# One run of value products per head pair, full-width sample products, and constant products ahead of the first slice, in a streaming encoder step

## The chip, the core and the metric

The kernel runs on one core of a Trainium2 chip. A core has a matrix engine (TensorE, shown as PE for its matmuls and PEld for its weight loads), three engines for elementwise work (VectorE or DVE, ScalarE or ACT, GpSimd or POOL) and an engine that issues transfers (SyncE or SP). TensorE reads on-chip memory and writes into PSUM, an accumulator memory of eight banks. The metric is the device time of one execution in microseconds.

## The reference

One inference step of one encoder layer, for 512 prompt frames and 64 new sample frames behind a cache of 128 frames. Width 1024, eight heads of 64 with a forget gate ("fox") and eight heads with an indexed sparse attention ("dsa"), a feed-forward width of 4096. Cut to what matters:

```python
h   = x @ w_in                       # q, k, v of both head groups, gates, index projections
# fox: s = q k^T / 8 + decay, causal, softmax, @ v
# dsa: the index heads score every key, the top 128 (sample: 48) keys are kept, softmax over them, @ v
x   = LN1(alpha * x + mix @ w_o)
x   = LN2(alpha * x + relu(x @ w_up)**2 @ w_down)
x   = x + sigmoid(x @ w_ple_gate + b) * (p @ w_ple)
```

The outputs are the new x of all frames and the new rows of the caches (k, v, log gates, index keys). The 64 sample frames attend to their 128 cached rows and to themselves: 192 keys. All of it is fp32.

## The kernel before

All activations lie transposed, features on the 128 partitions and the 576 frames (512 prompt, 64 sample) along a row. The large products are split: each fp32 operand is cast to a reduced format (fp32r, the high part), the rest is kept as a low part, and three fp32r products (high x high, low x high, high x low) take the place of one fp32 product. The function `gemm` emits these, in two halves of 288 frames; its matmuls stand at L278 for the whole kernel. The weights come by DMA in units of 512 KB, and ACT (L182) and DVE or POOL (L186) split them ahead of their use. Small products, such as transposes (L64) and the value products, are plain fp32, which the trace shows as two passes each, except for transposes, which are one.

**First stage** (`idx_main`). The inputs come in eight slices of 128 features: x (`xraw`), the index weights (`iraw`) and the first key weights (`WT.raw[0][0]`). `split_slice` casts and splits each slice on ACT, DVE and POOL (L394 to L403); then TensorE makes 6 matmuls for the first keys (L416) and 15 for the index projections (L423) per slice, 168 in all. The transfers are issued on SP in the order of the loop at L361 to L366; slice 0 comes in two halves of x.

**Attention.** The sixteen heads are worked as eight pairs: pairs 0 to 3 are fox, 4 to 7 dsa. While the projections of pair p + 1 run (`proj`, 3 units of 16 steps), the attention of pair p is woven in (`ticks`). A pair has nine jobs: for each block i of 128 queries and each of the two heads one prompt job (i + 1 key blocks), and one sample job for both heads. A job goes through the stages scores (`qk`), bias and maximum (`addmax`), exponential (`exp`), normalization, transposes of the weights (`ptrans`), their copy out of PSUM (`pevac`), value products (`pv`) and the output (`oevac`). The list `PLAN` gives each stage its lag in ticks behind the scores: `ptrans` 3, `pevac` 3, `pv` 4, `oevac` 5; within a tick the three lines of `PLAN` are separated by projection matmuls. `pv` runs only at a job that closes a group: at block 1 (queries 0 to 255: 4 products) and at block 3 (queries 256 to 511: 8 products), each into its half of the pair's PSUM bank `O` (tag "V", one buffer), and at the sample job. The transposed weights of blocks 0 and 1 lie in the tile `PT0`, those of blocks 2 and 3 in `PT1`, one buffer each.

The sample job has 64 queries of two heads, one head on each half of the partitions. Its scores are four fp32 products of 64 x 64 (L812, L813: cached and new keys, two heads), its values four products with 64 output rows (L898, L901).

Beside this, from the end of the first stage on, `choose` feeds DVE with the top-k choice of the sparse heads (logits L605 to L615, then maxima and replacements L635 and L637), until `chosen` covers pairs 4 to 7.

**Order.** The program order is that of the code; a planner in the compiler puts the instructions of each engine in order by the code's order and by when its own costs say that they are ready, and it sets the semaphores. Each engine, and each DMA queue, then runs strictly in that order.

The rest (output projection, LayerNorm, feed-forward, gate) follows from about 310 us on and is not edited.

Of the kernel before, what the change touches and what calls it, by code (L numbers as in the profile page):

```python
# [31 lines left out]
HW = NT // 2  # L32


@with_exitstack
def tile_hybrid_step(ctx: ExitStack, tc: tile.TileContext, I, O):
# [259 lines left out]

    cosT = sb.tile([128, NT], F32, name="cosT")
# [4 lines left out]
    def load_caches(g):  # L302
        KcT[g] = sb.tile([128, 4, 128], F32, name="KcT")
        Vc[g] = sb.tile([128, 512], F32, name="Vc")
        SP.dma_start(KcT[g], I["kcT"][g].rearrange("p (a t) -> p a t", a=4))
        SP.dma_start(Vc[g], I[("cache_fox_v", "cache_dsa_v")[g]][0, 0].rearrange("t h d -> t (h d)"))
# [54 lines left out]
    for a, b in ((0, 1), (1, 2), (2, 4), (4, 6), (6, 8)):  # L361
        SP.dma_start(xraw[:, a:b, :HW if a == 0 else NT], xT[:, a:b, :HW if a == 0 else NT])
        SP.dma_start(iraw[:, a:b], wix[:, a:b])
        if a == 0:
            SP.dma_start(xraw[:, 0, HW:], xT[:, 0, HW:])
        SP.dma_start(WT.raw[0][0][:, a:b], qkv[0][:, a:b])  # L366
# [284 lines left out]
    POOL.memset(zero, 0.0)  # L651
    for t in KLP:
        POOL.tensor_copy(t[64:128, 0], zero[64:128].to_broadcast([64, NP]))
        POOL.tensor_copy(t[0:64, 1], zero[0:64].to_broadcast([64, NP]))
    pair = {0: {}}

    def proj_evac(p, kind, m):
# [23 lines left out]
        if g == 0:  # L681
            if kind == "q":
                P["q32s"] = sb.tile([128, NS], F32, name="q32s", bufs=2)
# [15 lines left out]
                q(lambda: ACT.mul(P["q32s"], m[:, 1, HW - NS:HW], sc))  # L699
# [5 lines left out]
        else:  # L705
# [8 lines left out]
            if kind == "q":  # L714
                P["q32s"] = sb.tile([128, NS], F32, name="q32s", bufs=2)
                q(lambda: ACT.copy(QE[lo], x32[lo]), 5)
                q(lambda: ACT.copy(QO[hi], x32[hi]))
                q(lambda: DVE.tensor_tensor(QE[hi], x32[lo], f(QE[lo]), OP.subtract), 5)
                q(lambda: DVE.tensor_tensor(QO[lo], x32[hi], f(QO[hi]), OP.subtract))
                q(lambda: ACT.copy(P["q32s"], x32[:, NP:]))  # L720
                return
# [3 lines left out]
        P["k32s"] = sb.tile([128, NS], F32, name="k32s", bufs=2)  # L725
# [7 lines left out]
        q(lambda: ACT.copy(P["k32s"], k32[:, NP:]))  # L733
# [12 lines left out]
    def tok_out_s(src):  # L746
        m = psum_1("X", 1)
        transpose(m[:NS, 0:128], src[:, NP:], 128)
        return m
# [6 lines left out]
    def v_out(p):  # L756
        P, g = pair[p], p // 4
        m = tok_out(P["v32"])
        P["vt"] = sb.tile([128, 4, 128], F32, name="vtok", bufs=2)
        SP.dma_start(O["vT"][p // 4, p % 4], P["v32"])  # L760
        P["vs"] = sb.tile([NS, 128], F32, name="vs", bufs=2)
        ACT.copy(P["vt"], m.rearrange("p (b c) -> p b c", c=128))
        yield 1
        yield 1
        yield 1
        m = tok_out_s(P["v32"])
        ACT.copy(P["vs"], m[:NS, 0:128])

    def proj(p):
# [3 lines left out]
        for kind in "kqv" if p else "qv":  # L773
# [5 lines left out]
            if kind == "v" and p == 5:  # L779
                load_caches(1)  # L780
# [24 lines left out]
    def qk(j):  # L805
        P = pair[j["p"]]
        ps = psum_1("S", 1)
        if j["s"]:
            g, pp = divmod(j["p"], 4)
            for hh in range(2):  # L810
                r = slice(hh * 64, hh * 64 + 64)
                PE.matmul(ps[r, 0:PAST], P["q32s"][r], KcT[g][r, pp], start=True, stop=True)  # L812
                PE.matmul(ps[r, PAST:PAST + NS], P["q32s"][r], P["k32s"][r], start=True, stop=True)  # L813
# [45 lines left out]
    def ptrans(j):  # L859
        ps = psum_1("T", 1)  # L860
        j["T"] = ps
        if j["s"]:
            transpose(ps[:, 0:128], j["P"][:, 0:PAST], 128)
            transpose(ps[:NS, 128:256], j["P"][:, PAST:], 128)
        else:
            for b in range(j["i"] + 1):
                transpose(ps[:, b * 128:b * 128 + 128], j["P"][:, b * 128:b * 128 + 128], 128)
# [3 lines left out]
    def pevac(j):  # L871
        ps = j["T"]
        if j["s"]:
            t = sb.tile([128, 2, 128], F32, name="PTs")
            ACT.copy(t[:, 0], ps[:, 0:128])
            ACT.copy(t[:NS, 1], ps[:NS, 128:256])
# [3 lines left out]
        if i % 2 == 0 and hh == 0:  # L880
            pt_now["t"] = sb.tile([128, 2, 2 + 2 * (i // 2), 256], F32, name="PT", tag=f"PT{i // 2}")
        t = j["PT"] = pt_now["t"]
# [7 lines left out]
    def pv(j):  # L890
# [3 lines left out]
        if j["s"]:  # L894
            ps = j["O"] = psum_1("X", 1)
            g, pp = divmod(j["p"], 4)
            for hh, r in heads:
                PE.matmul(ps[r, :NS], Vc[g][:, (2 * pp + hh) * 64:(2 * pp + hh + 1) * 64], j["PT"][:, 0, r],  # L898
                          start=True, stop=False)
            for hh, r in heads:  # L900
                PE.matmul(ps[r, :NS], P["vs"][:, r], j["PT"][:NS, 1, r], start=False, stop=True)  # L901
            return
        i = j["i"]
        if i == 1:
            P["O"] = psum_1("V", 1)
        for kb in range(i + 1):
            c = slice(0 if kb < i else 128, 256)
            for hh, r in heads:
                PE.matmul(P["O"][r, (i - 1) * 128 + c.start:(i + 1) * 128], P["vt"][:, kb, r], j["PT"][:, hh, kb, c],  # L909
                          start=(kb == 0), stop=(kb == i))  # L910

    def oevac(j):
# [4 lines left out]
        ACT.copy(mx[:, NP:], j["O"][:, :NS])  # L917
# [167 lines left out]
    class LayerNorm:  # L1085
# [10 lines left out]
        def add(self, j):  # L1096
# [7 lines left out]
            else:  # L1104
                (DVE if j == 6 or self.sl is A else POOL).tensor_tensor(self.s, self.s, y[:, j:j + 2], OP.add)
            if j == 6:
                DVE.tensor_tensor(self.s[:, 0], self.s[:, 0], self.s[:, 1], OP.add)

# [449 lines left out]
```

## Time and profile before

| | |
|---|---|
| median of 3 runs | 798.68 us (798.48 to 799.44) |
| profiled execution | 798.88 us, span 797.2 us |
| TensorE matmuls, busy | 783.8 us (98%) |
| VectorE, busy | 539.4 us (68%) |
| ScalarE, busy | 430.3 us (54%) |
| GpSimd, busy | 119.0 us (15%) |
| DMA | 81.44 MB, mean 102 GB/s |

The span runs from the first to the last instruction that the profile shows; the execution's own time is 1.7 us longer. A TensorE share near 100% means that its instructions follow each other; how long a matmul takes from start to end is not what it costs, since matmuls overlap in the array. What one costs is read from the distance between starts.

### The profile page before, as it was taken

To read this page: it belongs to the slowest core of one execution; us is meant where nothing else is said; L and a number is where in the kernel's file an instruction comes from. 1 tells how busy PE (TensorE), PEld (TensorE's weight loads), DVE (VectorE), ACT (ScalarE), POOL (GpSimd) and SP (SyncE) were. 2 spreads that over 40 slices of the span, in tenths; PEclk is the share of its full clock that TensorE was granted. 3 is DMA by queue.
4 is the path that set the end of the run, shared out by engine and by line. 5 is a ranking of instruction groups with operands and counts; after the bars stand their busy time and mean duration, and the time that the engine had idled before them with its cause. 6 is when DMAs were issued, how large, how long until landed. Compare 5 with 4: busy or idle time off the path is not lost.

```text
span 797.2 us, 14908 instructions
## 1 busy us (share of the span) xinstructions
PE 783.8 (98%) x5886; PEld 755.7 (95%) x5886; DVE 539.4 (68%) x1100; ACT 430.3 (54%) x904; POOL 119.0 (15%) x117
## 2 busy tenths in 40 slices
PE   7999999999999999999999999999999999999997
PEld 7988898999999999999999999999999999999997
DVE  6679999644455654989856758577594765747643
ACT  5468656787677544588425427154271534616451
POOL 7202344354242000110000000000000000012200
PEclk9999999999999999999999999999999999999999
DMA  8537143354232223451313313142230513621001
GB/s 278 188 43 165 58 113 93 88 178 148 74 100 85 70 73 111 141 186 53 106 53 109 105 53 109 50 133 81 80 106 27 159 54 106 239 99 47 27 27 67
DMA packets 30358, 81.44 MB, mean 102 GB/s; under 512 B 5072, under 2 KB 9168, under 8 KB 30160
## 3 DMA queue, kind: packets, MB, share of 16 engines
q1 hardware_dynamic: 30288, 80.49, 32.9%
q8 instruction: 46, 0.75, 0.4%
q14 instruction: 24, 0.20, 0.1%
HBM read 66.38 MB, written 9.54 MB: 95 GB/s over the span
## 4 chain that ended last, share of the span: by engine, by line
PE 87%; DVE 8%; ACT 2%; DMA 1%; issue 1%; POOL 0%; SPq 0%; DVEq 0%; ACTq 0%
PE g L278 55%; PE m L278 18%; PE n L278 2%; DVE dbias L637 2%; PE V L909 2%; PE T L64 2%; DVE m L635 2%; PE S L822 1%; PE S L820 1%; PE m L416 1%; PE S L423 1%; PE X L64 1%; PE m L423 1%; DVE whl L186 1%; DVE dbias L615 1%
## 5 line engine op out<-in xcount | busy, mean ns | idle before, releaser
L182 ACT CAST whl<-wraw 128x512 fp32r<-128x512 f32 (+1 forms) x226 | 134.9, 611 | 170.7 <-PE g L278 145.6
L278 PE MATMUL g<-BH,whl 128*128 128x288 f32 (+2 forms) x864 | 181.5, 297 | 0.1
L278 PE MATMUL m<-AH,whl 128*128 128x288 f32 x736 | 178.3, 309 | 0.0
L186 DVE TENSOR_TENSOR whl<-wraw,whl 128x512 fp32r<-128x512 f32 (+1 forms) x192 | 130.0, 696 | 66.1 <-ACT whl L182 65.2
L278 PEld LDWEIGHTS g<-BH,whl 128*128 128x128 f32 x864 | 141.0, 188 | 2.3 <-ACT u L1322 1.2
L278 PEld LDWEIGHTS m<-AH,whl 128*128 128x128 f32 x736 | 126.2, 188 | 3.7 <-issue 2.2
L278 PE MATMUL g<-BL,whl 128*128 128x288 f32 (+2 forms) x432 | 127.4, 295 | 0.0
L278 PE MATMUL m<-AL,whl 128*128 128x288 f32 x368 | 109.0, 296 | 0.0
L278 PE MATMUL g<-hidE,whl 128*128 128x288 f32 (+2 forms) x768 | 103.4, 295 | 0.0
L278 PE MATMUL g<-hidO,whl 128*128 128x288 f32 (+2 forms) x768 | 103.3, 295 | 0.0
L278 PEld LDWEIGHTS g<-hidO,whl 128*128 128x128 f32 x768 | 102.3, 188 | 0.0
L278 PEld LDWEIGHTS g<-hidE,whl 128*128 128x128 f32 x768 | 102.2, 188 | 0.1
L278 PEld LDWEIGHTS g<-BL,whl 128*128 128x128 f32 x432 | 81.3, 188 | 0.1
L278 PEld LDWEIGHTS m<-AL,whl 128*128 128x128 f32 x368 | 69.5, 189 | 0.4
L278 PE MATMUL g<-s,whl 128*128 128x288 f32 x432 | 68.5, 298 | 0.0
L278 PEld LDWEIGHTS g<-s,whl 128*128 128x128 f32 x432 | 60.1, 188 | 2.2 <-DVE u L1324 1.1
L1103 POOL TENSOR_TENSOR ln_s<-Y 128x576 f32<-128x576 f32 (+2 forms) x3 | 5.0, 1665 | 381.7 <-DVE Y L1388 369.3
L838 ACT ACTIVATE sP<-sP,st 128x128 f32<-128x128 f32 (+4 forms) x72 | 39.6, 551 | 40.6 <-DVE st L830 40.2
L186 POOL TENSOR_TENSOR whl<-wraw,whl 128x512 fp32r<-128x512 f32 x34 | 44.1, 1297 | 86.8 <-ACT whl L182 68.9
L1363 DVE SCALAR_TENSOR_TENSOR Y<-Y,g 128x576 f32<-128x576 f32 x48 | 36.0, 750 | 21.7 <-PE g L278 21.2
L278 PE MATMUL m<-BH,whl 128*128 128x288 f32 x192 | 43.5, 304 | 0.0
L278 PEld LDWEIGHTS m<-BH,whl 128*128 128x128 f32 x192 | 32.1, 188 | 0.8 <-issue 0.5
(280 smaller groups left out, 1235.0 us busy)
## 6 DMA issues: line engine op xcount, KB each, us to landing
wraw<-in_w_up_dram SPq DMA_DIRECT2D x32, 512.0 KB, 3.5
wraw<-in_w_down_dram SPq DMA_DIRECT2D x32, 512.0 KB, 3.5
wraw<-in_w_qkv_dram SPq DMA_DIRECT2D x23, 512.0 KB, 3.8
wraw<-in_w_gate_dram SPq DMA_DIRECT2D x8, 512.0 KB, 4.1
wraw<-in_w_o_dram SPq DMA_DIRECT2D x8, 384.0 KB, 3.1
out_vT_dram<-v SPq DMA_DIRECT2D x8, 288.0 KB, 2.1
Y<-in_xT_dram SPq DMA_DIRECT2D x8, 288.0 KB, 5.1
PLD<-PL SPq DMA_DIRECT2D x4, 576.0 KB, 2.8
```

The source lines that it names most:

```text
L64: PE.transpose(out, in_, ident[:n, :n])
L182: ACT.copy(self.hv[h][0], src)
L186: eng.tensor_tensor(lv, src, f(hv), OP.subtract)
L278: PE.matmul(ps, W(w, kw, wc), a[:, ka, cols], start=(first and i == 0), stop=(last and i == n - 1))
L416: PE.matmul(mk[:, h, :HW], w0(part, k), a[:, k, h * HW:(h + 1) * HW], start=(k == 0 and i == 0), stop=(k == 7 and i == 2))
L423: PE.matmul(acc[b][:n[b], :304], a[:, k, b * 128:b * 128 + n[b]], ixw(part, k), start=(k == 0 and i == 0), stop=(k == 7 and i == 2))
L615: DVE.scalar_tensor_tensor(dst[:n, :nk], r[:n, :nk], w, dst[:n, :nk], op0=OP.mult, op1=OP.add)
L635: DVE.max(m, s)
L637: DVE.match_replace(out=s, in_to_replace=m, in_values=s, imm_value=GONE)
L838: ACT.activation(j["P"], j["P"], AF.Exp, bias=j["st"][:, 0:1], scale=-1.0, accum_out=s)
L909: PE.matmul(P["O"][r, (i - 1) * 128 + c.start:(i + 1) * 128], P["vt"][:, kb, r], j["PT"][:, hh, kb, c], start=(kb == 0), stop=(kb == i))
L1363: later(0, lambda y=y, m=m, s=s: DVE.scalar_tensor_tensor(y, y, s, m[:, :, :HW], op0=OP.mult, op1=OP.add))
```

## The change

Seven edits, in two groups.

*At the start:* eight fp32 products of the ones with themselves are emitted ahead of all else on TensorE, into the PSUM bank "V"; their result is not used. The transfers of slice 0's index weights and key weights are issued on ACT in place of SP.

*In the attention:*
- The prompt value products of both groups are made at block 3, as one run of 12, in place of 4 at block 1 and 8 at block 3.
- The sample scores are one product per pair: the queries of both heads stand in a 128 x 128 tile `QB` with zeros outside the two diagonal blocks, and the new keys are copied behind the cached ones in `KcT`, so that 192 keys are one operand.
- The sample values are two products of full width: the whole pair's columns of `Vc` and a 128-row tile `VS`, whose upper half is zero, against weights that are transposed 128 columns at a time. The second transpose covers keys 64 to 191; the rows of keys 64 to 127 meet the zeros of `VS`. Of the 128 x 128 result the two diagonal blocks are copied out, with one copy each.
- One copy takes both transposed blocks out of PSUM where there were two. The transpose of the sample's new values is 128 columns wide.
- `QB` and `VS` (two buffers each) are cleared once on POOL.
- `KcT` and `Vc` have two buffers, and the second cache load stands at the key unit of pair 4 in place of the value unit of pair 5.

```diff
+WARM = 8
...
+    warm = psum_1("V", 1)
+    for _ in range(WARM):
+        PE.matmul(warm[:, :128], ones, ones, start=True, stop=True)
...
     def load_caches(g):
-        KcT[g] = sb.tile([128, 4, 128], F32, name="KcT")
-        Vc[g] = sb.tile([128, 512], F32, name="Vc")
-        SP.dma_start(KcT[g], I["kcT"][g].rearrange("p (a t) -> p a t", a=4))
+        KcT[g] = sb.tile([128, 4, PAST + NS], F32, name="KcT", bufs=2)
+        Vc[g] = sb.tile([128, 512], F32, name="Vc", bufs=2)
+        SP.dma_start(KcT[g][:, :, :PAST], I["kcT"][g].rearrange("p (a t) -> p a t", a=4))
...
     for a, b in ((0, 1), (1, 2), (2, 4), (4, 6), (6, 8)):
+        other = ACT if a == 0 else SP
         SP.dma_start(xraw[:, a:b, :HW if a == 0 else NT], xT[:, a:b, :HW if a == 0 else NT])
-        SP.dma_start(iraw[:, a:b], wix[:, a:b])
+        other.dma_start(iraw[:, a:b], wix[:, a:b])
         if a == 0:
             SP.dma_start(xraw[:, 0, HW:], xT[:, 0, HW:])
-        SP.dma_start(WT.raw[0][0][:, a:b], qkv[0][:, a:b])
+        other.dma_start(WT.raw[0][0][:, a:b], qkv[0][:, a:b])
...
+    QB = [sb.tile([128, 128], F32, name=f"QB{x}") for x in range(2)]
+    VS = [sb.tile([128, 128], F32, name=f"VS{x}") for x in range(2)]
+    for t in QB + VS:
+        POOL.memset(t, 0.0)
...
-                q(lambda: ACT.mul(P["q32s"], m[:, 1, HW - NS:HW], sc))
+                q(lambda: (ACT.mul(QB[p % 2][lo, :NS], m[lo, 1, HW - NS:HW], sc),
+                           ACT.mul(QB[p % 2][hi, NS:], m[hi, 1, HW - NS:HW], sc)))
...
-                q(lambda: ACT.copy(P["q32s"], x32[:, NP:]))
+                q(lambda: (ACT.copy(QB[p % 2][lo, :NS], x32[lo, NP:]), ACT.copy(QB[p % 2][hi, NS:], x32[hi, NP:])))
...
-        q(lambda: ACT.copy(P["k32s"], k32[:, NP:]))
+        q(lambda: ACT.copy(KcT[g][:, pp, PAST:], k32[:, NP:]))
...
-        transpose(m[:NS, 0:128], src[:, NP:], 128)
+        transpose(m[:, 0:128], src[:, NT - 128:], 128)
...
-        ACT.copy(P["vs"], m[:NS, 0:128])
+        ACT.copy(VS[p % 2][NS:128], m[NS:128, 0:128])
...
-            if kind == "v" and p == 5:
+            if kind == "k" and p == 4:
                 load_caches(1)
...
-            for hh in range(2):
-                r = slice(hh * 64, hh * 64 + 64)
-                PE.matmul(ps[r, 0:PAST], P["q32s"][r], KcT[g][r, pp], start=True, stop=True)
-                PE.matmul(ps[r, PAST:PAST + NS], P["q32s"][r], P["k32s"][r], start=True, stop=True)
+            PE.matmul(ps[:, :PAST + NS], QB[j["p"] % 2], KcT[g][:, pp], start=True, stop=True)
...
-            transpose(ps[:NS, 128:256], j["P"][:, PAST:], 128)
+            transpose(ps[:, 128:256], j["P"][:, NS:PAST + NS], 128)
...
-            ACT.copy(t[:, 0], ps[:, 0:128])
-            ACT.copy(t[:NS, 1], ps[:NS, 128:256])
+            ACT.copy(t, ps[:, 0:256].rearrange("p (a c) -> p a c", a=2))
...
+            pair[j["p"]]["PT", i // 2] = pt_now["t"]
...
-            for hh, r in heads:
-                PE.matmul(ps[r, :NS], Vc[g][:, (2 * pp + hh) * 64:(2 * pp + hh + 1) * 64], j["PT"][:, 0, r],
-                          start=True, stop=False)
-            for hh, r in heads:
-                PE.matmul(ps[r, :NS], P["vs"][:, r], j["PT"][:NS, 1, r], start=False, stop=True)
+            PE.matmul(ps[:, :128], Vc[g][:, pp * 128:pp * 128 + 128], j["PT"][:, 0], start=True, stop=False)
+            PE.matmul(ps[:, :128], VS[j["p"] % 2], j["PT"][:, 1], start=False, stop=True)
             return
-        i = j["i"]
-        if i == 1:
-            P["O"] = psum_1("V", 1)
-        for kb in range(i + 1):
-            c = slice(0 if kb < i else 128, 256)
-            for hh, r in heads:
-                PE.matmul(P["O"][r, (i - 1) * 128 + c.start:(i + 1) * 128], P["vt"][:, kb, r], j["PT"][:, hh, kb, c],
-                          start=(kb == 0), stop=(kb == i))
+        if j["i"] < 3:
+            return
+        P["O"] = psum_1("V", 1)
+        for i in (1, 3):
+            t = P["PT", i // 2]
+            for kb in range(i + 1):
+                c = slice(0 if kb < i else 128, 256)
+                for hh, r in heads:
+                    PE.matmul(P["O"][r, (i - 1) * 128 + c.start:(i + 1) * 128], P["vt"][:, kb, r], t[:, hh, kb, c],
+                              start=(kb == 0), stop=(kb == i))
...
-        ACT.copy(mx[:, NP:], j["O"][:, :NS])
+        for hh in range(2):
+            r = slice(hh * 64, hh * 64 + 64)
+            ACT.copy(mx[r, NP:], j["O"][r, r])
```

More of the change, by code (lines that the diff above doesn't have):

```diff
@@ L682, in proj_evac @@
             if kind == "q":
-                P["q32s"] = sb.tile([128, NS], F32, name="q32s", bufs=2)
                 P["Q2"] = Q2[p % 2]
@@ L714, in proj_evac @@
             if kind == "q":
-                P["q32s"] = sb.tile([128, NS], F32, name="q32s", bufs=2)
                 q(lambda: ACT.copy(QE[lo], x32[lo]), 5)
@@ L724, in proj_evac @@
         P["KL"] = KL = KLP[p % 2]
-        P["k32s"] = sb.tile([128, NS], F32, name="k32s", bufs=2)
         q(lambda: ACT.copy(QE[lo], k32[lo]), 6 if g else 3)
@@ L760, in v_out @@
         SP.dma_start(O["vT"][p // 4, p % 4], P["v32"])
-        P["vs"] = sb.tile([NS, 128], F32, name="vs", bufs=2)
         ACT.copy(P["vt"], m.rearrange("p (b c) -> p b c", c=128))
```

## The prediction

> **What bounds the kernel now.** I read the page first, then the windows, then the timeline of the stretches that the change touches. The first two lines are the page's span and busy times; the other four are rows of the windows, whose columns are stretch, length, busy time and instructions of TensorE's matmuls (PE), its weight loads (PEld), VectorE (DVE), ScalarE (ACT), GpSimd (POOL), then clock, DMA share and GB/s.
>
> ```profile
> span 797.2 us, 14908 instructions
> PE 783.8 (98%) x5886; PEld 755.7 (95%) x5886; DVE 539.4 (68%) x1100; ACT 430.3 (54%) x904; POOL 119.0 (15%) x117
> 5.20:10.00 4.80, 4.71 (x17) 4.35 (x18) 3.76 (x4) 1.31 (x3) 4.35 (x6) 1.00 0.93 268
> 10.00:30.60 20.60, 20.60 (x151) 20.52 (x151) 12.93 (x16) 11.88 (x29) 12.84 (x17) 1.00 0.86 299
> 62.00:126.00 64.00, 61.19 (x454) 55.21 (x452) 62.53 (x181) 42.04 (x114) 21.27 (x19) 1.00 0.41 112
> 126.00:310.00 184.00, 184.00 (x1451) 170.92 (x1450) 102.97 (x266) 121.77 (x289) 56.54 (x46) 1.00 0.33 102
> ```
>
> TensorE is the bound, with two exceptions. From 62 to 126 us VectorE is busy for 62.5 of 64 us (the top-k choice): there TensorE waits for it now and then, and what TensorE saves is mostly lost. From 126 to 310 us TensorE is busy for all 184 us while ACT has 62 us and DVE 81 us free: there a microsecond less of TensorE is a microsecond less of the kernel. Behind 310 us nothing is edited, so that part only moves. The second exception is the clock at the start: 17 matmuls in 4.80 us (0.282 each) before 10.0 us, 151 in 20.60 (0.136 each) behind it, for the same shapes. The clock column says 1.00 in both rows; the matmul rate says that until about 10.0 us, 4.7 us after the first matmul, the array ran at half.
>
> **The start.** The timeline of the first microseconds (start, length, engine, line, operation; idle time before it and what ended it):
>
> ```profile
> 0.80 1.28 ACT L397 ACT_TABLE_LOAD   x1 [0.80 <-PEq L1536]
> 0.80 0.20 POOL L56 MEMSET ones<- 128x128 f32 x1 [0.29 <-POOLq L1536]
> 0.80 0.39 SPq L362 DMA_DIRECT2D xraw<-in_xT_dram  x1
> 1.25 0.42 SPq L363 DMA_DIRECT2D iraw<-in_w_idx_dram  x1
> 1.71 0.43 SPq L365 DMA_DIRECT2D xraw<-in_xT_dram  x1
> 3.03 0.43 ACT L397 CAST AH<-xraw 128x288 fp32r<-128x288 f32 x1 [0.95 <-DMA xraw<-in_xT_dram]
> 4.15 0.83 POOL L401 TENSOR_TENSOR iw<-iraw,iw 128x304 fp32r<-128x304 f32 x1 [1.74 <-DVE iw L398]
> 4.38 0.76 DVE L399 CAST AH<-xraw 128x288 fp32r<-128x288 f32 x1 [0.32 <-DMA xraw<-in_xT_dram]
> 5.29 0.59 PE L423 MATMUL S<-iw,AH 128*128 128x304 f32 x1 [5.29 <-DVE AH L399]
> 10.20 1.25 ACT L394 CAST AH<-xraw 128x576 fp32r<-128x576 f32 x2 [2.25 <-DMA xraw<-in_xT_dram]
> 11.35 0.45 ACT L395 CAST iw<-iraw 128x304 fp32r<-128x304 f32 x1
> ```
>
> *Two issues moved to ACT.* The first matmul waits for the second half of slice 0's x, whose issue stands third on SP (1.71) and becomes second (1.25): 0.46 us earlier. Its landing, the DVE cast and the first matmul follow: 5.29 becomes about 4.8. On ACT the two issues take some 0.8 us (two at 0.42), ahead of or behind the table load (1.28 from 0.80); ACT has 0.95 us idle before its first cast at 3.03, which covers them. If that cover were gone, the cast would be late by at most 0.8 us and the first matmul not before today's 5.29: a gain of 0, not a loss of size.
>
> *Eight constant products.* They need only the ones, ready at 1.00. How long they run cold is not in the trace; an fp32 product is two passes, and a full-width pass takes 0.111 us at full clock (rows below), so 16 passes take 1.8 us at that rate and 3.6 at twice it. They end between 2.8 and 4.7, before 4.8: nothing queues behind them that could run earlier.
>
> *What a warm array is worth.* The first two slices are 42 matmuls. Now 17 are done by 10.0 and 25 x 0.136 = 3.4 us follow: 13.4. With the full clock the third slice's data become the limit: its index weights are cast by 11.80 (11.35 and 0.45), behind a cast that waited 2.25 us for its DMA. The DMA share was 0.93 then, so earlier issues bring this forward by little; I take 0.3, so 11.5, a gain of at most 13.4 - 11.5 = 1.9. Starting at 4.8, 42 matmuls fit before 11.5 if the full clock is there by 6.7 us. If the products count as work, it comes 4.7 us after 1.0, so at 5.7. I take 1.8. Lower end: the clock still comes at 10.0, 5.2 / 0.282 = 18.4 matmuls are done by then, 23.6 x 0.136 = 3.2 follow, 13.2, a gain of 0.2; below that, cold passes of 0.3 us would end at 5.8 and cost up to 0.6. Upper end: 35 matmuls instead of 17 in the first 4.80 us, 18 x 0.136 = 2.4, and the 0.5 of the start: 2.9. From 30 to 62 us the chain is led by TensorE or by work that the end of this stage releases, so the gain reaches the DVE stretch and moves it forward whole.
>
> [...]
>
> The four new POOL clears (0.20 us each by the row of the ones) go into the 1.74 us that POOL idles before 4.15.
>
> **The value products.** Per pair there were two runs, one of 4 products (8 passes) and one of 8 (16 passes); now the first joins the second. Rows around a score step without a run, one with the short run, and two rows of the chain that give a run's length:
>
> ```profile
> 107.92 0.40 PE L822 MATMUL S<-KLP,fox 128*128 128x512 f32 x1
> ...
> 108.28 0.30 PE L278 MATMUL m<-AL,whl 128*128 128x288 f32 x1
> ```
>
> ```profile
> 111.09 0.40 PE L822 MATMUL S<-KLP,fox 128*128 128x512 f32 x1
> ...
> 111.42 0.87 PE L909 MATMUL V<-PT,vtok 128*64 128x256 f32 x8
> ...
> 112.46 0.29 PE L278 MATMUL m<-AL,whl 128*128 128x288 f32 x1
> ```
>
> ```profile
> 126.19 1.66 PE V L909 x16
> ...
> 141.96 0.80 PE V L909 x8
> ```
>
> From the score product to the projection's second matmul it is 0.36 us without and 1.37 us with the run: it costs 1.01. Its marginal cost in a longer run comes from the two lengths: 0.86 us for 8 passes more, 2048 columns more (3584 against 1536), so 0.42 ns per column and 0.645 for the short run's 1536. Joining saves 1.01 - 0.645 = 0.365 per pair, the array's switch into and out of half-width fp32 and back. If the joint saves only half the overhead it is 0.18.
>
> But the place matters: pair 1's short run (111.4) lies in the DVE stretch and its long run (126.2) behind it. In the TensorE-bound stretch six short runs go (pairs 2 to 7, 6 x 1.01 = 6.06) and seven long ones grow (7 x 0.645 = 4.52): 1.5.
>
> **The sample products.** Four 64-wide score products become one of full width and 192 columns (two passes); four value products become two of 128 columns (four passes). Now:
>
> ```profile
> 114.92 0.29 PE L278 MATMUL m<-AH,whl 128*128 128x288 f32 x1
> ...
> 115.14 0.44 PE L812 MATMUL S<-KcT,q32s 64*64 64x128 f32 x4
> ...
> 115.41 0.29 PE L813 MATMUL S<-k32s,q32s 64*64 64x64 f32 x4
> ...
> 115.86 0.30 PE L278 MATMUL m<-AL,whl 128*128 128x288 f32 x1
> ```
>
> ```profile
> 129.69 0.28 PE L822 MATMUL S<-KLP,fox 128*128 128x256 f32 x1
> ...
> 130.17 0.33 PE L901 MATMUL X<-PTs,vs 64*64 64x64 f32 x4
> ...
> 130.67 0.29 PE L278 MATMUL m<-AL,whl 128*128 128x288 f32 x1
> ```
>
> Two projection matmuls normally start 0.13 us apart (0.136 by the windows, with their slightly wider index products), so the scores cost 0.94 - 0.13 = 0.81; the value products 0.98 less 0.25 (0.36 with half the columns, 0.11 less) = 0.73. The new shapes are not in the trace; the nearest are full-width fp32 passes among fp32r matmuls, one transpose and ten passes of the gate sums:
>
> ```profile
> 211.18 0.29 PE L278 MATMUL m<-AH,whl 128*128 128x288 f32 x1
> 211.31 0.27 PE L64 MATMUL X<-ident,v 128*64 128x128 f32 x1
> ...
> 211.56 0.29 PE L278 MATMUL m<-AL,whl 128*128 128x288 f32 x1
> ```
>
> ```profile
> 43.80 0.29 PE L278 MATMUL m<-AH,whl 128*128 128x288 f32 x1
> ...
> 44.09 0.80 PE L558 MATMUL T<-LF,ones 128*128 128x24 f32 x6
> ...
> 45.18 0.30 PE L278 MATMUL m<-AL,whl 128*128 128x288 f32 x1
> ```
>
> One pass costs 0.38 - 0.13 = 0.25, ten (two, six and two) cost 1.38 - 0.13 = 1.25: 0.14 for the switch and 0.111 per pass. So the scores cost 0.14 + 2 x 0.111 = 0.36 (saving 0.45) and the values 0.14 + 4 x 0.111 = 0.58 (saving 0.15). Ends: passes exposed at 0.19, the length of one weight load, give 0.52 and 0.90 (saving 0.29, losing 0.17); passes at 0.42 ns a column give 0.30 and 0.35 (saving 0.51 and 0.38). I take the middle ones, the nearest rows. In the bound stretch lie six score and seven value products: 6 x 0.45 + 7 x 0.15 = 3.75 (0.5 to 5.7). The two transposes that grow from 64 to 128 columns cost nothing by the formula: the 64-wide one above already pays 0.25.
>
> [...]
>
> **The other engines.** Per pair ACT gets one more copy for the two halves of q and one more for the sample result, and one less for the transposed weights:
>
> ```profile
> L699 ACT ACTIVATE q32s<-m x4: 223/225/232, 45.2 to 139.4; 128x64 f32<-128x64 f32 x4
> L876 ACT COPY PTs<-T x8: 258/259/261, 96.0 to 306.0; 64x128 f32<-64x128 f32 x8
> ```
>
> That is about 0.2 us per pair, hidden under 62 us of free ACT time in the bound stretch; in the DVE stretch two pairs could lay 0.4 us on the chain; I take 0.1. The second cache load is issued a projection earlier into a buffer of its own; no matmul waited for the old one. DVE had 1.5 us idle in its stretch, and some of it may be waits for TensorE, which gets shorter there: I take 0.3, ends 0 and 1.5.
>
> **Sum.** 1.8 (start) + 1.5 (joined runs) + 3.75 (sample) + 0.3 - 0.1 = 7.3 us. The profiled execution took 798.88 (span 797.2 and 1.7 around it), 0.2 above the median of 798.68, so it stands for the median: 798.9 - 7.3 = 791.6. Its own range, from the neighbouring values, is 789.5 to 793.
>
> **Rivals.**
> - *The clock still comes at 10.0.* The constant products end up to 2 us before the first slice, and nothing here shows how much gap the grant bears; today 4.7 us of unbroken work came before it. The start gives 0.2: 798.9 - 5.7 = 793.2.
> - *Another engine takes over from 126 us on.* TensorE's zero idle time hides how close the next engine is. Against it stands ACT at 66% and DVE at 56%; for it, that score buffers turn over through both in order. If half of the 5.25 us and half of the 1.8 are left: 798.9 - 3.5 = 795.4.
> - *VectorE's stretch shrinks too,* by its whole 1.5 us of idle time: 798.9 - 8.5 = 790.4.
> - *The joined run comes too late for its buffer.* The first transposed weights of a pair now stay until the run at the pair's end, and have one buffer; if the order of instructions puts the next pair's transposes ahead of the run, the evacuation (L886, L888) waits on ACT or DVE with the weight casts and exponentials behind it. The run is 0.645 + 1.66 = 2.3 us, over seven pair changes up to 16. From 1.05 us per change on the gain of 7.3 is gone; priced at two thirds of the run, 1.6 us, it is 7 x 1.6 = 11.2, less 7.3, 3.9 slower: 802.8. Against it: in the code's order the run stands one tick, some 3 us, ahead of that evacuation.
> - *It does nothing that reaches the end:* the array waits elsewhere for what it saves, 798.
>
> **How the numbers follow.** Forecast 0.48, late clock 0.20, another engine 0.14, the shorter DVE stretch 0.08, the buffer 0.06, nothing 0.04. A measurement of this kernel can tell 0.2%, 1.6 us, from no change. Faster: 0.48 + 0.20 + 0.14 + 0.08 = 0.90; same 0.04; slower 0.06. The range 788.5 to 796.0 takes in the first four with the ends of the sample products and leaves out the last two and the tails.
>
> **What would show it.** Matmuls of the first 25 us at 0.136 already by 7 us and the third slice's start at 11.5; one value run of 24 passes and 2.3 us per pair, none of 8; two passes of score products in 0.36 us; TensorE still without a wait from about 124 us on. Wrong would be: a matmul rate of 0.28 until 10 us, waits of TensorE for DVE or ACT behind 126 us, or evacuations that wait for the value run.

## The result, and the profile after

The changed kernel takes 794.2 us in the median of four runs (794.15 to 795.54), the kernel before 798.7 (798.48 to 799.44). The ratio is 0.9946, with a 95% interval of 0.9929 to 0.9963: faster by 4.5 us. Forecast were 791.6, with a range of 788.5 to 796.0. The direction and the range held; 2.6 of the 7.1 us against the median are missing, and the experiments say where.

The page of the kernel after: its span and its busy times.

```profile
span 793.8 us, 14800 instructions
PE 780.9 (98%) x5822; PEld 759.0 (96%) x5822; DVE 539.4 (68%) x1100; ACT 434.0 (55%) x912; POOL 119.4 (15%) x121
```

TensorE has 64 matmul passes fewer (80 fewer in the sample products, 16 more at the start) and 2.9 us less busy time. The profiled execution is the slowest of the four, 795.54; the other three took 794.15 to 794.25. What the profiles show of the two groups is told under the clock, below.

**Where the time went, in the profiles.** The last index product of the first stage starts at 30.61 us before and at 30.95 after: in this execution the start gained nothing. From there to the end it is 766.6 us before and 762.9 after, so 3.7 us of gain in the attention; of the 4.5 us this leaves 0.8 for the first stage. The value runs show in which pair it came. First the chain of waits before, then after; each row is the start, the length and the passes of a pair's long run, pair 1 first:

```profile
126.19 1.66 PE V L909 x16
155.48 1.66 PE V L909 x16
184.79 1.66 PE V L909 x16
...
243.38 1.66 PE V L909 x16
274.26 1.66 PE V L909 x16
```

```profile
126.40 2.31 PE V L912 x24
155.72 2.31 PE V L912 x24
184.05 2.31 PE V L912 x24
...
240.72 2.31 PE V L912 x24
271.07 2.31 PE V L912 x24
```

A run of 24 passes takes 2.31 us, as forecast. From pair 2 to pair 3 the distance falls from 29.31 to 28.33, by 0.98 us where 0.96 were forecast. But from pair 1 to pair 2 it is 29.29 before and 29.32 after, although the forecast counted that pair too, and from pair 5 to pair 6 only 0.53 us are saved (30.88 to 30.35).

**The first stage.** It lost something too. Slice 0's low part (what is left of x beside its high part) comes later, first before, then after:

```profile
5.24 1.02 DVE L402 TENSOR_TENSOR AL<-xraw,AH 128x576 fp32r<-128x576 f32 x1
...
6.32 0.61 PE L416 MATMUL m<-AL,whl 128*128 128x288 f32 x1
```

```profile
5.22 3.54 DVE L408 TENSOR_TENSOR AL<-xraw,AH 128x576 fp32r<-128x576 f32 x2
...
5.59 0.82 POOL L407 TENSOR_TENSOR iw<-iraw,iw 128x304 fp32r<-128x304 f32 x1
...
7.09 0.61 PE L422 MATMUL m<-AL,whl 128*128 128x288 f32 x1 [0.23 <-DVE AL L408]
```

DVE starts at the same time but takes 1.82 us for the first of its two instructions in place of 1.02, and the first low product starts at 7.09 in place of 6.32. Beside it POOL splits the index weights, which it did at 4.15 before: with the new clears the planner puts four casts that fill `KLP`, a tile of the attention (0.61 us each, from 3.04), ahead of that split. The prediction let the clears go into POOL's idle time at no cost. Why DVE is slower here is not shown: with the sample products alone POOL has the same order, and DVE takes 0.98.

The new products, in the timeline after, one step of scores and one of values:

```profile
202.63 0.29 PE L279 MATMUL m<-AH,whl 128*128 128x288 f32 x1
202.77 0.48 PE L817 MATMUL S<-KcT,QB 128*128 128x192 f32 x2
...
203.22 0.29 PE L279 MATMUL m<-AL,whl 128*128 128x288 f32 x1
```

```profile
216.56 0.28 PE L826 MATMUL S<-KLP,qO 128*128 128x256 f32 x1
216.67 0.38 PE L901 MATMUL X<-PTs,Vc 128*128 128x128 f32 x2
216.89 0.39 PE L902 MATMUL X<-PTs,VS 128*128 128x128 f32 x2
...
217.25 0.29 PE L279 MATMUL m<-AL,whl 128*128 128x288 f32 x1
```

By the prediction's way of counting the scores cost 0.59 - 0.13 = 0.46 us (forecast 0.36, before 0.81) and the values 0.69 - 0.25 = 0.44 (forecast 0.58, before 0.73). The two score passes start 0.16 us apart: the forecast had priced a pass of 192 columns at 0.111 us, from a row of 128 columns and narrow ones such as 24. For the values the four passes of 0.11 us are all that is seen, without the 0.14 for a switch. By luck the two deviations nearly cancel.

**What holds pair 2.** TensorE waits again, just before pair 2's run. The timeline after, rows of ACT, DVE and TensorE:

```profile
150.97 0.34 DVE L643 MATCH_REPLACE8 dbiasS<-m,dbiasS 64x192 f32<-64x192 f32 x1
...
151.41 0.44 ACT L645 ACTIVATE dbiasS<-dbiasS,big 64x192 f32<-64x192 f32 x1
...
151.88 0.35 ACT L647 COPY dbiasS<-dbiasS 64x192 f32<-64x192 f32 x1
...
152.26 0.58 ACT L769 COPY vtok<-X 128x512 f32<-128x512 f32 x1
...
152.90 0.33 PE L65 MATMUL X<-ident,v 128*128 128x128 f32 x1 [0.57 <-ACT vtok L769]
```

The value transposes that `vtok` copies out of PSUM stood ready at 149.2 us (they start at 148.53 and take 0.63). The copy comes at 152.26, because ACT's order has the last mask of the top-k choice ahead of it, in two instructions (L645 and L647). The first cannot start before the last top-k round on VectorE has ended (150.97 + 0.34), and starts at 151.41, right behind an exponential. Before, the masks stood ahead of the copy too (the second at 151.36, the copy at 151.73), but TensorE came to its transpose only at 152.72, when the copy was done.

### The profile page after: what moved, and what is told of

It reads as the page before. It is cut to its first block, busy times and chain, and to the rows that moved or that the text cites. A ratio compares the mean times of both kernels' runs of the same rounds, so it can differ in the third digit from the quotient of the medians.

```text
span 793.8 us, 14800 instructions
## 1 busy us (share of the span) xinstructions
PE 780.9 (98%) x5822; PEld 759.0 (96%) x5822; DVE 539.4 (68%) x1100; ACT 434.0 (55%) x912; POOL 119.4 (15%) x121
## 4 chain that ended last, share of the span: by engine, by line
PE 80%; DVE 10%; issue 5%; ACT 2%; POOL 1%; DMA 1%; SPq 0%; DVEq 0%; ACTq 0%; POOLq 0%
PE g L279 55%; PE m L279 13%; PE n L279 2%; DVE dbias L643 2%; DVE m L641 2%; PE V L912 2%; PE T L65 1%; DVE dbias L621 1%; PE m L422 1%; PE X L65 1%; PE m L429 1%; PE S L826 1%; PE S L429 1%; PE S L824 1%; DVE sP L834 1%
## 5 line engine op out<-in xcount | busy, mean ns | idle before, releaser
L183 ACT CAST whl<-wsum 128x512 fp32r<-128x512 f32 x24 | 14.8, 617 | 32.9 <-PE g L279 32.7
```

The costliest lines, as they stand in the source:

```text
L183: ACT.copy(self.hv[h][0], src)
```

## The experiments

Each is compared with the kernel before, measured beside it on the same chip. Where two kernels are set against each other by their profiles, the comparison is made from the last index product on, so that the clock of the start has no part in it.

### The start alone

```diff
+    warm = psum_1("V", 1)
+    for _ in range(WARM):
+        PE.matmul(warm[:, :128], ones, ones, start=True, stop=True)
...
+        other = ACT if a == 0 else SP
```

> Before, with the start group alone (eight constant products, two issues of slice 0 on ACT). Theory A (the choice on VectorE holds TensorE until it ends at about 151 us, so what TensorE saves up to there is lost; the start itself gives little, because the constant products do not bring the full clock earlier and slice 0 does not land earlier): 797.7 to 799.0, first matmul still near 5.3 us, matmuls at half rate until about 10 us where the clock comes late. Rival B (the attention gave its whole forecast 5.4 us and the start lost 0.9 of it): 799.6 or more. The prediction's own 1.8 us: 796.9.

Measured: 797.59 us against 798.97, ratio 0.9986 (0.9977 to 0.9995): 1.4 us. The eleven runs lie in two groups, seven at 797.08 to 797.78 and four at 798.51 to 799.07. Rival B is out: the start costs nothing. Theory A is half right: the profiled execution, of the late group, starts its first index product at 5.51 and shows no gain, but most executions do gain. The prediction's 1.8 was near.

### The attention alone

The kernel after, without the start's two edits:

```diff
-    warm = psum_1("V", 1)
-    for _ in range(WARM):
-        PE.matmul(warm[:, :128], ones, ones, start=True, stop=True)
...
-        other = ACT if a == 0 else SP
+        other = SP
```

> Before, with the attention group alone (no constant products, all issues on SP). Theory A: the gain begins at about 151 us, five short value runs and the sample products of pairs 3 to 7: 3.6 to 4.2 us, 794.6 to 795.1; TensorE waits for ACT or DVE around 148 to 155 us. Rival B: 5.3 to 5.6 us, 793.2.

Measured: 795.92 us, ratio 0.9959 (0.9945 to 0.9972): 3.05 us. From the last index product on the profile has 763.0 us, 3.6 less than before, as theory A had it; the run of pair 2 comes 29.32 us behind that of pair 1 here too. Start and attention add up: 1.4 + 3.05 = 4.45. The 0.5 us between 3.6 and 3.05 is lost in the first stage, as far as a median of runs tells that scatter by 1.9 us: here too the first low product starts at 7.09, and TensorE waits 0.74 us for it.

### The joined runs alone, the sample products alone

```diff
-        if i == 1:
-            P["O"] = psum_1("V", 1)
...
+        if j["i"] < 3:
+            return
+        P["O"] = psum_1("V", 1)
+        for i in (1, 3):
```

> Before, with the joined value runs alone. Theory A: five short runs (5 x 1.01) go behind 151 us and six long runs grow (6 x 0.645): 1.2 us, 797.5. The prediction's 126 us as the end of the VectorE stretch: 1.5 us, 797.2. If joining saves nothing but the place of the run: 798.7.

Measured: 797.12 us, ratio 0.9974 (0.9963 to 0.9984): 1.85 us, and 1.9 us by the profile from the last index product on, more than theory A's 1.2 and the prediction's 1.5. The distance from pair 2 to pair 3 is 28.96 us, 0.35 less than before, as the prediction had it per pair.

```diff
-            for hh in range(2):
-                r = slice(hh * 64, hh * 64 + 64)
-                PE.matmul(ps[r, 0:PAST], P["q32s"][r], KcT[g][r, pp], start=True, stop=True)
-                PE.matmul(ps[r, PAST:PAST + NS], P["q32s"][r], P["k32s"][r], start=True, stop=True)
+            PE.matmul(ps[:, :PAST + NS], QB[j["p"] % 2], KcT[g][:, pp], start=True, stop=True)
```

> Before, with the sample products of full width alone (scores, values, their copies, caches in two buffers). In the profile after, a pair's scores cost 0.46 (0.81 before) and its values 0.44 (0.73). Theory A: 5 x 0.35 + 6 x 0.29 = 3.5 us at most, 795.2 to 796.0. Rival B (bound from 126 us on): 6 x 0.35 + 7 x 0.29 = 4.1 us, 794.6.

Measured: 795.85 us, ratio 0.9962 (0.9949 to 0.9974): 3.1 us; 2.95 by the profile. The time lies in theory A's range. Its distance from pair 2 to pair 3 is 28.69 us, 0.62 less than before. The rows of the chain, first the joined runs, then the sample products (pairs 1 to 3):

```profile
125.21 2.31 PE V L912 x24
154.20 2.31 PE V L912 x24
183.16 2.31 PE V L912 x24
```

```profile
126.54 1.66 PE V L905 x16
155.40 1.66 PE V L905 x16
184.09 1.66 PE V L905 x16
```

Alone, the two parts seem to save time up to pair 2 (28.99 and 28.86 us against 29.29), and 1.85 and 3.1 make 4.95, more than the 3.05 of both together. The intervals overlap, but the profiles say the same: 1.9 + 2.95 = 4.85 against 3.6.

The distance between two runs tells a saving only if the first of them has not moved. Counted from the last index product (at 30.61 us before, 30.16 with the joined runs alone, 30.53 with the sample products alone, 30.95 after), pair 2's run starts 124.87 us later before, 124.04 with the joined runs alone, 124.87 with the sample products alone, and 124.77 after. So up to there the joined runs alone save 0.83 us, the sample products alone save nothing (their pair 1 comes 0.43 us later, which makes the distance shorter), and both together save 0.10. The orders on ACT differ: with the joined runs alone the second mask (L641, at 151.28) stands behind the value copy (L762, at 150.69), and TensorE does not wait for the copy. The 0.73 us lost here, and 0.47 from pair 5 to pair 6 (0.34 and 0.66 saved alone, 0.53 together), make up the difference between 4.85 and 3.6.

### A shorter choice

```diff
-            for r in range(16 if i < 4 else 6):
+            for r in range(6 if i < 4 else 2):
```

This was made in the kernel before and in the kernel after. A round finds eight keys, so the choice keeps 48 and 16 keys where the reference keeps 128 and 48; nothing else is left out.

> Before, with 6 of the 16 and 2 of the 6 top-k rounds of the choice left in (the choice keeps the wrong number of keys; 34 rounds of some 1.1 us less on VectorE). Theory A: VectorE's stretch ends before about 115 us, some 36 us of VectorE work go, but TensorE is close behind it, so the time falls by only 1 to 4 us: 795 to 798.

> After, with the same shortened choice. Theory A (savings up to 151 us are lost to the choice): the distance to the shortened before grows from 4.5 to about 6.5 us or more (0.96 per pair for two pairs more). Rival (the missing gain is lost elsewhere): the distance stays at 4.5.

Measured: 797.83 us before and 791.45 after, 6.4 us apart (4.5 with the full choice). The four runs after lie in two groups, at 790.7 and 792.2, so the 6.4 depends on their mix; from the last index product on it is 765.0 against 759.5, 5.5 us in place of 3.7. Theory A holds. The chain of the shortened kernel after, pairs 0 to 3:

```profile
94.11 2.31 PE V L912 x24
122.42 2.31 PE V L912 x24
150.73 2.31 PE V L912 x24
179.06 2.31 PE V L912 x24
```

Every distance up to pair 5 is 28.3 us now, from pair 0 on; before, shortened, they are 29.3 (95.83, 125.12 and 154.41). With the choice out of the way these pairs save their 0.97 us each. From pair 5 to pair 6 only 0.52 us are saved here too (30.88 to 30.36), so the choice has no part in that loss.

### The last mask later

```diff
+            if i == 4:
+                for _ in range(8):
+                    yield 0.5
             ACT.activation(s, s, AF.Relu, bias=big[:n, 0:1])
```

> After, with the last two mask instructions of the choice (L645 and L647, the sample part) emitted some 6 us later, so that on ACT they no longer stand ahead of pair 2's value copy while they wait for VectorE's last top-k round at 151 us. Theory A1 (pair 2's saving of 0.96 us is lost because TensorE's transposes at 152.9 wait for that copy behind those masks): about 0.6 to 0.9 us less than after, 793.3 to 793.7, and the run of pair 2 starts 0.6 to 0.9 us nearer to the run of pair 1 than the 29.32 us of after. Rival A2 (VectorE itself is the bound up to there): 794.2, the distance stays 29.3.

Measured: 794.2 us, ratio 0.9941 (0.9924 to 0.9957), distance 29.31. This decides nothing: the order of instructions shows the mask on ACT in the same place, two ahead of the value copy. Emitting it later in the code did not move it. The run is still of use: it has the kernel after's order on TensorE and ACT, and its profiled execution is one of the early group.

### The last mask on VectorE

```diff
-            ACT.activation(s, s, AF.Relu, bias=big[:n, 0:1])
             if i == 4:
-                ACT.copy(dbiasS[64:128], dbiasS[0:64])
+                DVE.tensor_scalar(s, s, 2e38, 0.0, op0=OP.add, op1=OP.max)
+                DVE.tensor_copy(dbiasS[64:128], dbiasS[0:64])
+            else:
+                ACT.activation(s, s, AF.Relu, bias=big[:n, 0:1])
```

> After, with the choice's last mask (the sample part, L645 and L647) made on VectorE, right behind its last top-k round, so that ACT waits for it no more and pair 2's value copy is free. Theory A1 (TensorE's 0.6 us wait at 152.9 for that copy, behind the masks in ACT's order, is where pair 2's saving goes): the wait is gone, the value run of pair 2 starts 28.4 to 28.8 us behind that of pair 1 instead of 29.3, and the kernel takes 0.5 to 0.9 us less than after. Rival A2 (the stretch is bound by VectorE or by the score buffers whatever ACT's order is): distance 29.3, same time as after.

Measured: 793.50 us (three runs at 793.35 to 793.50, two at 794.93 and 794.99), ratio 0.9936 (0.9923 to 0.9948): 0.7 us less than after. The chain, pairs 1 to 3:

```profile
126.46 2.31 PE V L914 x24
154.98 2.31 PE V L914 x24
183.31 2.31 PE V L914 x24
```

The distance from pair 1 to pair 2 is 28.52 us in place of 29.32, and the copy starts at 151.47, right behind the exponential, without the masks. From the last index product on it is 762.2 us against 762.9. Theory A1 is confirmed: 0.8 us of pair 2's saving was lost to what stood ahead of the copy in ACT's order. It is just the length of the two mask instructions, 0.44 and 0.35 us. As they leave ACT altogether, this run does not tell their place in the order from their time.

### Wide constant products

```diff
-    for _ in range(WARM):
-        PE.matmul(warm[:, :128], ones, ones, start=True, stop=True)
+    POOL.memset(causal, 1.0)
+    for _ in range(4):
+        PE.matmul(warm, ones, causal, start=True, stop=True)
```

> After, with four constant products of 512 columns in place of eight of 128 (their operand is the causal tile, filled with ones beforehand, which delays them by some 0.3 us). Theory C1 (the narrow passes, 0.236 us each cold for 128 columns, keep the array less than half at work, so in some executions they do not count for the clock): the full clock comes before about 8 us in every execution and the times lie close together, 793.0 to 793.9. [...]

Measured: 798.56 us, ratio 0.9991 (0.9981 to 1.0). The experiment failed in its aim: as the tile has to be filled first, the planner put the products behind ten of slice 0's matmuls, and TensorE was held there:

```profile
7.76 0.46 PE L429 MATMUL S<-iw,AL 128*64 128x304 f32 x1
8.01 4.93 PE L315 MATMUL V<-causal,ones 128*128 128x512 f32 x8
...
12.37 0.83 PE L422 MATMUL m<-AH,whl 128*128 128x288 f32 x2
```

They take 4.4 us from the index products, and the kernel is 4.4 us slower than after. These are not the same 4.4: after gains 1.2 to 1.7 us by its early products, and against the kernel without any (795.90, below) the loss is 2.7. So work put into the first stage costs time there, but less than its full length.

```diff
+        PE.matmul(warm.rearrange("p (a c) -> p a c", a=4), ones, ones[:, None, :].to_broadcast([128, 4, 128]),
+                  start=True, stop=True)
```

> After, with four constant products of 512 columns (the ones read four times) in place of eight of 128, first in TensorE's order. Theory C1 (the narrow passes keep the array at work for less than half of the time and therefore count in some executions only): the full clock comes at 7.4 us or before in every execution, and the times lie within 0.5 us of each other at 793.6 to 794.2. [...] Eight passes of 512 columns at half clock take about 3.5 us, so the first index product should not be later than 5.3.

Measured: 794.78 us (794.73 to 795.25), ratio 0.9947 (0.9934 to 0.9959). The five runs lie within 0.5 us and the index products have the full rate from the start (0.13 to 0.14 us apart from 7.49 on), as theory C1 had it, but at a price: eight passes take 6.46 us, not the 3.5 that the author estimated (by the prediction's 0.42 ns per column, at half rate, 3.44; they start 0.853 us apart), the first product is late, and the times lie 0.6 us above the early ones of after.

```profile
1.06 6.46 PE L300 MATMUL V<-ones 128*128 128x512 f32 x8 [1.06 <-POOL ones L57]
6.96 0.69 PE L423 MATMUL m<-AH,whl 128*128 128x288 f32 x1
7.49 0.30 PE L423 MATMUL m<-AL,whl 128*128 128x288 f32 x1
7.62 0.30 PE L430 MATMUL m<-iw,AH 128*128 128x304 f32 x1
```

The longer and unbroken work may be the cause as well as the width, so width alone is not shown. Nor is it shown that narrow passes keep the array less at work: at half clock the passes of 128 columns start 0.213 us apart and those of 512 columns 0.853, the same time per column.

### The attention with the two issues

The kernel after without the eight products, so the issues on ACT are all that it has beyond the attention alone:

```diff
-    warm = psum_1("V", 1)
-    for _ in range(WARM):
-        PE.matmul(warm[:, :128], ones, ones, start=True, stop=True)
```

> After, without the constant products: the two issues on ACT stay. Theory: the issues bring nothing (the first index product started at 5.27 after and 5.29 before), so this equals the attention group alone, 795.9, times spread over 1.5 us with the phase of the clock. The prediction's 0.5 us for the earlier issue: 795.4.

Measured: 795.90 us, ratio 0.9958 (0.9944 to 0.9971), the same as the attention alone (795.92). The first index product starts at 5.28. What the expectation calls the phase of the clock is the time at which the clock becomes full, which differs from execution to execution (10.03 us in the profile of before; here the matmuls run 0.22 us apart until 12.4 us and 0.135 behind it). The issues on ACT bring nothing that can be told from the scatter (794.41 to 797.15 here); the start's gain is that of the constant products, 1.7 us from here to after (1.2 with each set against the kernel before beside it, 799.25 and 798.73).

### Nine constant products and the mask on VectorE

```diff
-WARM = 8
+WARM = 9
```

The mask stands on VectorE as in the diff above.

> After, with the last mask on VectorE and nine constant products in place of eight, so that they end near 5.1 us, where the first index product can start at 5.3. Theory D (the constant products do release the clock; TensorE's idle time between 4.7 and 7.1 us, 0.6 before the first index product and 1.1 at the low part of slice 0, withholds or takes it back in some executions): fewer executions fall into the later group, which lies 1.4 us higher; 793.3 to 793.6 in four of five or more. [...] The mask alone accounts for 0.75 us against after in both groups.

Measured: 793.39 us, ratio 0.9933 (0.9919 to 0.9946), all five runs between 793.37 and 793.43. None falls into the later group. With eight products 18 of 28 runs of five kernels are early, so five early ones in a row would come by chance about one time in nine: this speaks for theory D, but does not prove it. This is the fastest of the kernels that keep all the reference's keys, 0.8 us below after, and the steadiest.

## The clock

The profile of the kernel with the last mask on VectorE shows the clock become full, fall back and become full again. Four stretches of its first 14.5 us (columns: stretch, length, busy time and count of PE, PEld, DVE, ACT and POOL, then clock, DMA share and GB/s):

```profile
1.00:4.30 3.30, 3.24 (x15) 3.24 (x16) 0.17 (x1) 1.66 (x2) 3.04 (x15) 1.00 0.73 208
4.30:7.70 3.40, 1.88 (x12) 1.42 (x12) 3.26 (x4) 1.57 (x5) 3.30 (x6) 1.00 1.00 354
7.70:11.10 3.40, 3.40 (x16) 3.36 (x15) 3.40 (x6) 2.79 (x7) 1.91 (x3) 0.51 1.00 371
11.10:14.50 3.40, 3.40 (x26) 3.38 (x25) 3.40 (x5) 2.94 (x8) 3.40 (x5) 0.99 1.04 401
```

The clock column counts from the first time at which the clock is recorded as full and says 1.00 ahead of it; in the first row the passes start 0.213 us apart, the half rate. The trace's own record of the clock has it full from 4.36 us, half from 7.77 and full again from 11.18, two steps of 3.41 us. So the clock was full for 3.41 us. In the second row, which covers nearly that stretch, TensorE was busy for 1.88 of 3.40 us; the third row has a clock of 0.51 and 16 matmuls where the fourth has 26. The timeline of the same execution shows the idle time and the rates:

```profile
1.06 3.61 PE L300 MATMUL V<-ones 128*128 128x128 f32 x16 [1.06 <-POOL ones L57]
5.29 0.38 PE L429 MATMUL S<-iw,AH 128*128 128x304 f32 x1 [0.62 <-DVE AH L405]
5.50 0.30 PE L429 MATMUL X<-iw,AH 128*128 128x304 f32 x1
...
5.92 0.30 PE L429 MATMUL S<-iw,AH 128*64 128x304 f32 x1
7.12 0.40 PE L422 MATMUL m<-AL,whl 128*128 128x288 f32 x1 [0.90 <-DVE AL L408]
...
8.01 0.46 PE L429 MATMUL m<-iw,AH 128*128 128x304 f32 x1
8.26 0.68 PE L422 MATMUL m<-AH,whl 128*128 128x288 f32 x2
```

There are 0.62 us of waiting before slice 0 and 0.90 at its low part. The first products run 0.14 us apart, those behind 8 us 0.25. With nine products the waits shrink to nothing before slice 0 and 0.35 at the low part, and the full rate is there from 7.3 us on (21 matmuls between 7.30 and 10.00; the profile after has its matmuls at half rate until 10.4). The time at which the clock becomes full differs from execution to execution, and in two profiled executions the groups go with it: the record has the full clock from 6.55 us in the early execution of the later mask and from 10.37 in the late one of after, and the last index product starts at 29.48 and 30.95, 1.46 us apart. Without constant products the record has it between 8.0 and 12.5 us (six profiled executions; 10.03 in before). This fits the spread of before, 798.2 to 799.8 in nearly all runs, but was not followed run by run.

What brings the full clock, and what takes it back, is not shown. With the same eight constant products, begun at 1.06 us, the clock became full at 4.36, 6.55 and 10.37 us in three executions. In the last of them, the profile after, TensorE was busy for 3.25 us of the first of these stretches and for 2.74 of the second, 3.24 and 1.88 in the execution above, and 3.24 and 3.05 with nine products, where the clock is recorded as full from 6.49 us on. In the third stretch after has 17 matmuls, the execution above 16 and the kernel with nine products 27. That a gap of some 0.4 us ahead of the first product can decide it is the author's estimate, from the five early runs with nine products and the waits in these profiles.

## Why the prediction was right and wrong

- **The start, 1.8 us:** the constant products came near it (1.4 with the start alone; 1.7 as the difference of 795.9 and 794.2, or 1.2 with each set against the kernel before beside it), but the first stage as a whole gained only the 0.8 that are left beside 3.7. The attention edits slow it, by 0.2 to 0.5 as far as the medians tell. The prediction put the POOL clears, the edit of theirs that runs there, at nothing; the low part of slice 0 comes 0.77 us later with them, but how they do it is not shown. The first step was wrong too: the issues on ACT did not bring slice 0 forward. x landed later (ACT's first cast at 3.58, before 3.03), and DVE's cast of the index weights took 0.70 us, before 0.32, with POOL busy beside it; with the sample products alone POOL is busy there as well and the cast takes 0.32, so the cause is open. The products take 3.78 us, just beyond the long end of the 1.8 to 3.6 forecast. The rival "the clock still comes at 10.0" was not a matter of the kernel but of the execution: it happened in one run of four.
- **"From 126 us on a microsecond less of TensorE is a microsecond less of the kernel":** this step failed. It was read from TensorE's zero idle time between 126 and 310. The choice on VectorE goes on to 151 us, and what waits behind it on ACT set pair 2's run. Counted from pair 1's run to pair 2's, 0.96 us were forecast and -0.03 measured; moving the mask gave 0.80 of it back. That is the rival "another engine takes over", in one place in place of all: not through ACT's load over the stretch, which the prediction weighed (62 us free), but through what stands ahead of one copy in its order. The prediction's own sign of being wrong, a wait of TensorE for ACT behind 126 us, is in the profile after.
- **Pair 5 to 6:** 0.96 forecast, 0.53 measured. Of the missing 0.43, 0.23 are a wait of TensorE for the copy of v on ACT at 261.7, which neither part alone has; the rest was not followed.
- **The VectorE stretch:** 0.3 less 0.1 for ACT forecast; from the last index product to pair 1's run it is 0.13 us shorter.
- **The joined runs:** 0.365 per pair forecast, 0.35 measured alone; their place (pair 1's long run grows behind the stretch) was right.
- **The sample products:** together 0.60 per pair forecast, 0.64 by the costs above and 0.62 with the sample products alone. The prediction's row of four passes at 115.14 is a merged one: in the trace of before the passes of the two heads start 0.013 us apart (115.140 and 115.153, then 115.300 and 115.313), those of the values 0.007. So the old products ran two at once. Their cost (0.81 and 0.73) had been read from the rows around them, so the forecast did not depend on it.
- **The buffer of the first transposed weights:** no evacuation (L890, L892) waits for the value run, only for its own transposes; the rival did not happen.

Sum from the last index product on: 5.45 forecast; less 1.0 (pair 2), 0.4 (pair 6), 0.1 (up to pair 1) and 0.3 behind the start of pair 7's run (0.5 to be lost there by the forecast, for its own growth, and 0.8 measured), 3.7. With 0.8 in place of 1.8 in the first stage this makes the 4.5.

## What to carry to other kernels

A bound engine without idle time says nothing on how close the next limit is: before a saving is counted, look for what else ends just ahead of each of its waits, above all an instruction in another engine's order that waits for a third one. Here the saving came back by moving two instructions, 0.79 us together, to the engine whose result they needed anyway. Work that only keeps the array busy gave the steadiest times here where it reached up to the first real product without a gap (nine products: 793.37 to 793.43 in five runs). It should be ready before anything else: in the first run of wide products it was not, and the planner put it behind ten of slice 0's matmuls, where it took 4.4 us from the index products. And a merged row of a timeline gives the time of its instructions together, not whether they ran one by one.

## What was not expected of the hardware

- A plain fp32 pass at half clock took twice its time at full clock, and its time went by its columns. In the first run of wide products the passes of 512 columns start 0.853 us apart until the clock becomes full at 10.68, and 0.429 behind it; the passes of 128 columns start 0.213 apart at half clock. Reading the operand four times over makes no difference: 0.853 again.
- Half-width passes of two heads ran at once: in a value run after, they start in pairs 0.006 us apart, and the pairs of 256 columns follow each other every 0.216 us, about the time that one full-width pass would take by the 0.429 for 512 columns.
- In one execution the clock became full at 4.36 us, while the constant passes ran, and fell back to half at 7.77, 3.41 us later, behind 3.40 us in which TensorE was busy for 1.88 (the clock, above).
